# Two transformer blocks on one core: held weight chunks, a later norm product, and later down groups

## The chip, the core and the metric

The kernel runs on one core of a Trainium2 chip. The core has five engines that work side by side, each through its own list of instructions in order: PE (TensorE, the matrix products), DVE (VectorE), ACT (ScalarE), POOL (GpSimd) and SP (SyncE, which here issues the weight transfers). They wait for one another through semaphores. Matrix products are written to PSUM, eight banks of 512 fp32 columns; everything else lies in SBUF. The metric is the device time of one execution in microseconds (us).

## The reference, cut to what matters

Input: x of 256 tokens by 1024 features, fp32. Two different blocks follow each other, each two layers deep:

```
first block, per layer:
  x = x + concat(diff_attention, moba_attention)(rms_norm(x) @ w_in) @ w_out
  x = x + (silu(g) * up) @ w_down,   g, up = split(causal_conv3(rms_norm(x) @ w_up))
second block, per layer:
  x = x + 0.5 * (silu(h @ w_gate) * (h @ w_up)) @ w_down,   h = rms_norm(x)
  x = x + merged @ w_out     # forgetting attention and a gated linear recurrence, both
                             # from rms_norm(x) @ w_in, each gated by a sigmoid
  x = x + 0.5 * (the same feed-forward with other weights)
rms_norm(x) = x * rsqrt(mean(x^2) + 1e-6) * g
```

The feed-forward is 2816 wide in both blocks (22 pieces of 128). There are ten norms and six feed-forwards in all.

## The kernel before, in words

**Layout and products.** Activations are kept feature-major: X is four tiles that hold eight pieces of 128 features by 256 tokens. Each fp32 operand is split in two halves, high (rounded to the fast fp32 format) and low (the rest), and a product is two or three matmuls: high by high, high by low, low by high. The weight's high half (wh) is made by ScalarE, the low half (wl) by VectorE as raw minus wh. Names of tiles, as the profile shows them: raw, wh, wl for weights; xs for a norm's split input; as for a feed-forward's split activation; x for X; sq for the norm's squares and their running sum; st for the product that sums over features; rstd for the norm's factor; mm, mv and acc for PSUM banks of a projection, of a q/k/v projection with tokens as rows, and of a down contraction.

**The weight stream.** All weights are one list of chunks in the order of use (`phase_chunks`, line 176 on). A chunk is 128 by 1024 (one kind is slightly wider). `issue_dma` brings it into one of 7 raw buffers, `piece_h` and `piece_l` convert it in two halves of 512 columns into one of 5 buffers each for wh and wl (`RING = 5`). `next_chunk` takes the next one for use: it sets `st["done"]` to that chunk, and `h_open` lets a conversion be put in only for chunks below

```python
return c < st["dma"] and c < st["done"] + RING
```

so a chunk five further on, which goes into the same buffer, is opened only when the current one has moved on. What is put into an engine's list before the buffer is free waits there for the last matmul that reads it.

**The order of work.** It is written out when the kernel is built. A class `Estimate` keeps for each engine a planned time `T[engine]` and for each tile the time `R[tile]` at which it is planned ready. The main line issues PE's products; after each pair of matmuls `substep` runs `urgent` (weights that are nearly due), `tick` (units of background work: each is a generator that yields the engine and the tiles it waits for, and goes on once they are planned ready) and `fill` (conversions ahead). So a planned ready time decides where in PE's list a unit's matmuls stand. The real engines then run the lists in order.

**Norms.** `boundary` (line 720 on) is called as each piece of a residual sum is complete: it adds the piece to X, makes the split input of the next norm (`norm_tile`: high half on ScalarE, low half on VectorE), squares it on ScalarE and adds the square to the running sum on POOL (for the first norm on VectorE). After the eighth piece `norm_tail` (line 485 on) puts the two st matmuls into PE's list, once the sum is planned ready, and then the factor rstd = rsqrt (ScalarE and VectorE) and, where tokens must be scaled, two transposes (rt). The projections do not wait for rstd, since it is applied when a bank is emptied.

**Feed-forward.** `ffn` walks the order that `ffn_order(lag)` gives. "up" is a projection by two chunks, whose result is emptied, gated and split into an as tile. "dn" is one group of the down contraction: two as tiles by one chunk, into four of the eight output pieces (the first half). The groups of the first half come between the ups, each `lag` ups behind; the second half's groups come after all ups, and its last two groups are taken together. `lag` is 4 in the first block and 2 in the second.

**The last contraction.** In `down` and `down2` the last step takes its two chunks at once, as a list, and goes over the output pieces in the outer loop, so that pieces become complete one after the other:

```python
w = list(k_chunks(n, len(groups)))
for m in range(4):
    for i, h, l_ in w:
        one(i, m, h, l_)
```

By then `next_chunk` has been called twice, so `st["done"]` is the second chunk, while the first is read up to the last piece.

Of the kernel before, what the change touches and what calls it, by code (L numbers as in the profile page):

```python
# [144 lines left out]
def kernel(ctx: ExitStack, tc: tile.TileContext, t: dict):  # L145
    nc = tc.nc
    ctx.enter_context(tc.manual_schedule())
    est = Estimate()
# [31 lines left out]
    def phase_chunks():  # L180
        for l in range(L):
            wo = t["w_out"]
            at = {"dq0": 0, "dq1": 1, "mq0": 2, "mq1": 3, "dv0": 4, "mv0": 5}
            for step in MIX1.split():
                if step[1] == "o":
                    halves(wo[l, 2 * (step[0] == "m") + int(step[2])])
                else:
                    for i in range(2):
                        halves(t["w_p1"][l, at[step], i])
            ffn_chunks(t["w_up"], t["w_down"], l, 4)  # L190
        for l in range(L):
            ffn_chunks(t["w_gu1"], t["w_d1"], l, 2)
            wi = t["w_in2"]
            base = {"q": 0, "k": 4, "v": 8, "x": 12, "r": 16, "a": 20, "n": 24}
            for step in MIX2.split():
                if step == "q0":
                    halves(t["w_qf"][l])
                elif step == "G":
                    halves(t["w_g"][l])
                elif step in PAIRS:  # L200
                    for i in range(2):
                        halves(t["w_p2"][l, PAIRS.index(step), i])
                elif step[0] == "O":
                    half, g = divmod(int(step[1]), 2)
                    stream.extend(half_rows(t["w_out2"][l], half, 2 * g + i) for i in range(2))
                elif step[0] in "AR":
                    halves(t[{"A": "w_oa", "R": "w_or"}[step[0]]][l, int(step[1])])
                else:
                    halves(wi[l, base[step[0]] + int(step[1])])
            ffn_chunks(t["w_gu2"], t["w_d2"], l, 2)  # L210

    def halves(a):
        w = a.shape[-1] // 2
        stream.extend(a[:, i * w:(i + 1) * w] for i in range(2))
# [19 lines left out]
    def ffn_chunks(u, d, l, lag):  # L234
        for what, j in ffn_order(lag):
            if what == "up":
                halves(u[l, j])
            else:
                stream.extend(half_rows(d[l], j[0], g) for g in j[1])
# [14 lines left out]
    st = {"dma": 0, "h": 0, "l": 0, "use": 0, "done": 0}  # L254
# [90 lines left out]
    def W(eng, *aps):  # L345
        return (eng, aps)
# [138 lines left out]
    def norm_tail(N):  # L485
        while N.ss is None or N.ss[1] < KT:
            yield POLL
        ssum = N.ss[0]
        yield W("pe", ssum)
        while not bank_ok():  # L490
            yield POLL
        b = bank("st")
        pe.matmul(b[:, :S], ones_d, ssum, start=True, stop=True)
        yield W("act", b)
        r = blk("rstd")[:, :S]
        yield from rsqrt(r, b[:, :S], S)
        N.rstd = r
        if N.tok:

            yield W("pe", r)  # L500
            while not bank_ok():
                yield POLL
            b = bank("rt")
            for tt in range(2):
                pe.transpose(b[:, tt * P:(tt + 1) * P], r[:, tt * P:(tt + 1) * P], ident)
            yield W("dve", b)
            rt = small(4, "rt")
            dve.tensor_copy(rt[:, 0:2], b[:, 0:S:P])
            unbank()
            N.rt = rt  # L510

            yield W("dve", rt)
            dve.tensor_mul(rt[:, 2:4], rt[:, 0:2], rt[:, 0:2])
            yield W("dve", rt)
            dve.reciprocal(rt[:, 2:4], rt[:, 2:4])
            yield W("dve", rt)
            dve.tensor_scalar_mul(rt[:, 2:4], rt[:, 2:4], EPS)
            N.e2 = rt[:, 2:4]
# [55 lines left out]
    def k_chunks(n=KT, c=2):  # L574

        per = n // c
        for i in range(c):
            h, l_ = next_chunk(None)
            h3 = h.rearrange("p (k c) -> p k c", k=per)
            l3 = l_.rearrange("p (k c) -> p k c", k=per)  # L580
            for j in range(per):
                yield i * per + j, h3[:, j], l3[:, j]

    def proj(R):

# [82 lines left out]
    def down(acc, R, first, last, after=None):  # L668

        def one(k, m, h, l_):  # L670
            ms = slice(m * P, (m + 1) * P)
            mm3(as2(acc[m // 2])[:, m % 2], h[:, ms], l_[:, ms], R.high(k), R.low(k),
                first and k == 0 and m % 2 == 0, last and k == 1 and m % 2 == 1)

        if not last:
            for k, h, l_ in k_chunks(2):
                for m in range(KT):
                    one(k, m, h, l_)
                    substep()
        else:  # L680
            w = list(k_chunks(2))
            for p in range(4):
                for k, h, l_ in w:
                    for m in (2 * p, 2 * p + 1):
                        one(k, m, h, l_)
                        if k == 0:
                            substep()
                after(2 * p, [as2(acc[p])[:, 0]], False)
                after(2 * p + 1, [as2(acc[p])[:, 1]])
                substep()  # L690

    def down2(acc, R, groups, half_, first, last, after):

        n = 2 * len(groups)

        def one(i, m, h, l_):
            ms = slice(m * P, (m + 1) * P)
            mm2(acc[m], h[:, ms], l_[:, ms], R.both(2 * groups[i // 2] + i % 2), first and i == 0, last and i == n - 1)

        if not last:  # L700
            for i, h, l_ in k_chunks(n, len(groups)):
                for m in range(4):
                    one(i, m, h, l_)
                    substep()
        else:
            w = list(k_chunks(n, len(groups)))
            for m in range(4):
                for i, h, l_ in w:
                    one(i, m, h, l_)
                    if i < n - 1:  # L710
                        substep()
                after(4 * half_ + m, [hi(acc[m]), lo(acc[m])])
                substep()
# [24 lines left out]
    def ffn(N, evac, scale, N2, lag, mul):  # L738
        R = Ops(N.X)
        A = Ops([None] * NF)  # L740
        acc = [[], []]
        for what, j in ffn_order(lag):
            if what == "up":
                b = mul(R)
                spawn(evac(N, b if mul is proj else summed("u", b), j, A.tiles))
                substep()
            else:
                half_, groups = j
                wait_for(lambda: all(A.tiles[2 * g + i] is not None for g in groups for i in range(2)))
                first = not acc[half_]  # L750
                if first:
                    wait_for(lambda: bank_any(4))
                    acc[half_] = [bank("acc") for _ in range(4)]
                down2(acc[half_], A, groups, half_, first, NG - 1 in groups, boundary(scale, N2))
# [776 lines left out]
    norms = []  # L1531
# [7 lines left out]
    with tc.tile_pool(name="b1pool", bufs=1) as bp:  # L1539
        N0 = norms[0]  # L1540
        C = block1_consts(bp, N0)
        T.update(pe=T0 - 300.0, act=T0 - 700.0, dve=T0 - 200.0, pool=5000.0)
        for k in range(KT):
            a = blk("xs", F32R)
            act.activation(hi(a), xt(k), AF.Identity, scale=v1(N0.g, k))
            dve.scalar_tensor_tensor(lo(a), xt(k), v1(N0.g, k), hi(a).bitcast(F32), op0=ALU.mult, op1=ALU.subtract)
            piece_h()
            piece_l()
            N0.X[k] = a
        T["pe"] = T0 + 2000.0  # L1550
        for k in range(KT):
            add_squares(N0, squares(k))
        spawn(norm_tail(N0), front=True)
        for l in range(L):
            if l == 1:
                spawn(consts2())
            mix1(l, norms[2 * l], C, norms[2 * l + 1])
            ffn(norms[2 * l + 1], make_evac_conv(l), 1.0, norms[2 * l + 2], 4, proj)
    with tc.tile_pool(name="b2pool", bufs=1) as bp:
        C = block2_consts(bp)  # L1560
        for l in range(L):
            o = 4 + 3 * l
            ffn(norms[o], evac_swiglu, 0.5, norms[o + 1], 2, proj2)
            mix2(l, norms[o + 1], C, bp, norms[o + 2])
            ffn(norms[o + 2], evac_swiglu, 0.5, norms[o + 3], 2, proj2)
    wait_for(lambda: not active)


# [121 lines left out]
```

## Time and profile before

| what | value |
|---|---|
| time, median of three runs | 1904.14 us (1903.15 to 1908.57) |
| the profiled execution's own time | 1904.0 us |
| its span, first to last instruction | 1902.2 us |
| PE busy | 1865.8 us |
| DVE busy | 1534.8 us |
| ACT busy | 1271.2 us |
| POOL busy | 63.5 us |
| mean granted TensorE clock | 0.995 |

Busy time is the union of an engine's instructions; waiting is not in it. Nearly every instruction shows line 112, that of the helper which records it, so the tiles' names tell the work apart. "Idle before" in a row is the time the engine stood still just before the instruction, with the engine, line and tile that ended the wait.

### The profile page before, as it was taken

The numbers are of one execution on the slowest core, as the hardware profiler recorded it, in microseconds if no ns is written. First come the engines' busy times: TensorE is split into PE (matmuls) and PEld (weight loads), VectorE is DVE, ScalarE is ACT, GpSimd is POOL, SyncE is SP. The second block draws the span as 40 slices with busy tenths as digits, with TensorE's granted clock in tenths as the row PEclk, the third lists the DMA queues.
The fourth block names the chain that finished last, engine by engine and source line by source line (L and its number), as shares of the span: only waits on it lengthen the run. The fifth ranks groups of instructions, "written<-read, shape, count | busy, mean of one in ns | idle before, by whom it ended". The sixth has DMA issues, their size and how long they took to land.

```text
span 1902.2 us, 32094 instructions
## 1 busy us (share of the span) xinstructions
PE 1865.8 (98%) x11446; PEld 1657.9 (87%) x11446; DVE 1534.8 (81%) x3284; ACT 1271.2 (67%) x3099; POOL 63.5 (3%) x91
## 2 busy tenths in 40 slices
PE   9999999999999999999999999999999999999998
PEld 7899997889999888888888888888888888888887
DVE  7879886888988777779969877767776898898775
ACT  7866665876666666567788666556655778866653
POOL 2010001001000000000000100010001000000000
PEclk9999999999999999999999999999999999999999
DMA  9446655444655566655556566656666455565662
GB/s 288 150 144 194 188 182 160 138 153 135 210 186 175 182 188 188 189 193 162 157 177 192 187 191 187 186 169 190 187 185 210 157 161 172 189 197 188 189 188 82
DMA packets 113153, 339.76 MB, mean 179 GB/s; under 512 B 10796, under 2 KB 11860, under 8 KB 112480
## 3 DMA queue, kind: packets, MB, share of 16 engines
q1 hardware_dynamic: 111392, 330.21, 55.4%
q0 software_dynamic: 1456, 7.47, 1.4%
q8 instruction: 90, 1.47, 0.3%
q14 instruction: 71, 0.58, 0.1%
q10 hardware_dynamic: 144, 0.02, 0.0%
HBM read 336.30 MB, written 1.36 MB: 178 GB/s over the span
## 4 chain that ended last, share of the span: by engine, by line
PE 89%; DVE 7%; ACT 2%; DMA 1%; issue 1%; POOL 0%; POOLq 0%; SPq 0%; ACTq 0%
PE mm L112 49%; PE acc L112 22%; PE mv L112 12%; DVE wl L112 2%; PE av L112 2%; PE s L112 1%; DMA raw<-in_w_p 1%; ACT wh L112 1%; DVE x L112 1%; PE qt L112 1%; PE pt L112 1%; PE g L112 1%; DVE xs L112 1%; DVE z L112 0%; PE st L112 0%
## 5 line engine op out<-in xcount | busy, mean ns | idle before, releaser
L112 DVE TENSOR_TENSOR wl<-raw,wh 128x512 fp32r<-128x512 f32 x1248 | 819.1, 688 | 216.6 <-ACT wh L112 192.4
L112 ACT ACTIVATE wh<-raw 128x512 fp32r<-128x512 f32 x1248 | 718.3, 628 | 317.0 <-PE mm L112 101.7
L112 PE MATMUL mm<-xs,wh 128*128 128x256 f32 (+1 forms) x2816 | 753.4, 340 | 6.8 <-DVE xs L112 4.8
L112 PE MATMUL mm<-xs,wl 128*128 128x256 f32 x2112 | 596.7, 283 | 0.0
L112 PEld LDWEIGHTS mm<-xs,wh 128*128 128x128 f32 x2816 | 485.5, 190 | 70.0 <-DVE xs L112 6.5
L112 PEld LDWEIGHTS mm<-xs,wl 128*128 128x128 f32 x2112 | 401.2, 190 | 0.2
L112 PE MATMUL acc<-as,wh 128*128 128x512 f32 x1056 | 372.4, 394 | 5.4 <-DVE as L112 5.4
L112 PE MATMUL acc<-as,wl 128*128 128x256 f32 x1056 | 297.1, 281 | 0.0
L112 PE MATMUL mv<-wh,xs 128*128 128x512 f32 (+2 forms) x832 | 255.8, 388 | 0.4 <-DVE xs L112 0.4
L112 PEld LDWEIGHTS acc<-as,wh 128*128 128x128 f32 x1056 | 198.2, 188 | 51.5 <-DVE as L112 7.3
L112 PEld LDWEIGHTS acc<-as,wl 128*128 128x128 f32 x1056 | 198.7, 188 | 0.0
L112 PE MATMUL mm<-hS,wh 128*128 128x512 f32 x512 | 180.9, 395 | 0.0
L112 PEld LDWEIGHTS mv<-wh,xs 128*128 128x128 f32 x832 | 149.9, 191 | 28.2 <-DVE xs L112 0.8
L112 PE MATMUL mv<-wl,xs 128*128 128x512 f32 (+2 forms) x416 | 157.8, 379 | 0.0
L112 PE MATMUL mm<-hS,wl 128*128 128x256 f32 x512 | 143.9, 281 | 0.0
L112 ACT ACTIVATE u<-mm 128x256 f32<-128x256 f32 x176 | 63.9, 383 | 92.1 <-PE mm L112 92.0
L112 DVE TENSOR_TENSOR u<-mm,u 128x256 f32<-128x256 f32 x176 | 67.8, 423 | 61.5 <-ACT u L112 61.3
L112 PEld LDWEIGHTS mm<-hS,wh 128*128 128x128 f32 x512 | 96.1, 188 | 21.1
L112 POOL TENSOR_TENSOR sq<-sq,sq 128x256 f32<-128x256 f32 x63 | 50.2, 797 | 1578.4 <-ACT sq L112 1577.1
L112 PEld LDWEIGHTS mm<-hS,wl 128*128 128x128 f32 x512 | 96.4, 188 | 0.1
L112 PEld LDWEIGHTS mv<-wl,xs 128*128 128x128 f32 x416 | 79.4, 191 | 14.8
L112 DVE SCALAR_TENSOR_TENSOR y<-u,vec,y 128x255 f32<-128x255 f32 (+1 forms) x176 | 80.8, 481 | 3.1
(210 smaller groups left out, 2225.6 us busy)
## 6 DMA issues: line engine op xcount, KB each, us to landing
raw<-in_w_gu SPq DMA_DIRECT2D x176, 512.0 KB, 4.3
raw<-in_w_up SPq DMA_DIRECT2D x88, 512.0 KB, 4.1
raw<-in_w_d SPq DMA_DIRECT2D x88, 512.0 KB, 4.4
raw<-in_w_p SPq DMA_DIRECT2D x84, 512.0 KB, 4.6
raw<-in_w_in SPq DMA_DIRECT2D x68, 512.0 KB, 3.7
raw<-in_w_down SPq DMA_DIRECT2D x44, 512.0 KB, 4.1
raw<-in_w_out SPq DMA_DIRECT2D x32, 512.0 KB, 4.2
raw<-in_w_oa SPq DMA_DIRECT2D x16, 512.0 KB, 4.0
```

The costliest lines, as they stand in the source:

```text
L112: f(*a, **k)
```

## The change

It has three parts. The order `ffn_order` is asked for with a lag of 6 instead of 4 in the first block and of 4 instead of 2 in the second, in the list of chunks and in the walk alike. In `norm_tail` the running sum's planned ready time is raised by 1500 ns before the unit waits for it, so that the st matmuls stand later in PE's list. And the two places that take their chunks as a list do so by a new function, which sets `st["done"]` back to the first of them until the next chunk is called for.

```diff
-            ffn_chunks(t["w_up"], t["w_down"], l, 4)
+            ffn_chunks(t["w_up"], t["w_down"], l, 6)
...
-            ffn_chunks(t["w_gu1"], t["w_d1"], l, 2)
+            ffn_chunks(t["w_gu1"], t["w_d1"], l, 4)
...
-            ffn_chunks(t["w_gu2"], t["w_d2"], l, 2)
+            ffn_chunks(t["w_gu2"], t["w_d2"], l, 4)
...
         ssum = N.ss[0]
+        est.R[ssum.name] += 1500.0
         yield W("pe", ssum)
...
+    def held_chunks(n, c):
+
+        first = st["use"]
+        w = list(k_chunks(n, c))
+        st["done"] = first
+        return w
...
-            w = list(k_chunks(2))
+            w = held_chunks(2, 2)
...
-            w = list(k_chunks(n, len(groups)))
+            w = held_chunks(n, len(groups))
...
-            ffn(norms[2 * l + 1], make_evac_conv(l), 1.0, norms[2 * l + 2], 4, proj)
+            ffn(norms[2 * l + 1], make_evac_conv(l), 1.0, norms[2 * l + 2], 6, proj)
...
-            ffn(norms[o], evac_swiglu, 0.5, norms[o + 1], 2, proj2)
+            ffn(norms[o], evac_swiglu, 0.5, norms[o + 1], 4, proj2)
...
-            ffn(norms[o + 2], evac_swiglu, 0.5, norms[o + 3], 2, proj2)
+            ffn(norms[o + 2], evac_swiglu, 0.5, norms[o + 3], 4, proj2)
```

## Rows read from the trace of the kernel before

**Rows 1.** The page's first two parts: busy time, and tenths in 40 slices.
```profile
PE 1865.8 (98%) x11446; PEld 1657.9 (87%) x11446; DVE 1534.8 (81%) x3284; ACT 1271.2 (67%) x3099; POOL 63.5 (3%) x91
...
PEclk9999999999999999999999999999999999999999
```

**Rows 2.** Waits of PE: engine, tile, waited for: us in total, times, longest us.
```profile
PE st L112 <- POOL sq L112: 12.8, 7, 2.4
PE acc L112 <- DVE as L112: 5.4, 6, 1.1
PE mm L112 <- DVE xs L112: 4.8, 6, 1.2
PE mm L112 <- DVE sp L112: 2.6, 2, 1.3
PE mm L112 <- ACT xs L112: 2.0, 2, 1.0
...
PE qt L112 <- DVE qn L112: 2.0, 2, 1.7
PE mv L112 <- DVE xs L112: 0.4, 2, 0.2
PE rt L112 <- DVE rstd L112: 0.3, 1, 0.3
```

**Rows 3.** Timeline of PE, 634 to 641: start us, duration us, instruction [idle before].
```profile
634.04 0.39 PE L112 MATMUL mm<-xs,wh 128*128 128x512 f32 x1
...
637.04 0.28 PE L112 MATMUL mm<-xs,wl 128*128 128x256 f32 x1
637.16 0.40 PE L112 MATMUL mm<-xs,wh 128*128 128x512 f32 x1
...
638.97 0.28 PE L112 MATMUL mm<-xs,wl 128*128 128x256 f32 x1
640.87 0.70 PE L112 MATMUL st<-sq,cst 128*128 128x256 f32 x2 [1.62 <-POOL sq L112]
```

**Rows 4.** Windows: stretch, length, busy by engine, PEclk, DMA share, GB/s.
```profile
130.80:134.10 3.30, 3.30 (x16) 3.30 (x17) 3.30 (x8) 2.27 (x7) 2.40 (x4) 0.50 0.00 0
...
1274.20:1277.50 3.30, 3.30 (x13) 2.82 (x12) 2.22 (x5) 3.27 (x7) 0.00 (x0) 0.50 0.57 168
```

**Rows 5.** Timeline of ACT over the same boundary.
```profile
633.42 1.15 ACT L112 ACTIVATE wh<-raw 128x512 fp32r<-128x512 f32 x2 [3.74 <-PE acc L112]
...
639.06 0.51 ACT L112 ACTIVATE xs<-x,vec 128x256 fp32r<-128x256 f32 x1 [0.37 <-DVE x L112]
```

**Rows 6.** Timeline of DVE over the same boundary.
```profile
638.15 0.88 DVE L112 TENSOR_TENSOR x<-acc,x 128x256 f32<-128x256 f32 x2
```

**Rows 7.** Groups of instructions: count | busy us, mean ns | idle before, releasers.
```profile
L112 DVE TENSOR_TENSOR wl<-raw,wh 128x512 fp32r<-128x512 f32 x1248 | 819.1, 688 | 216.6 <-ACT wh L112 192.4 <-PE acc L112 14.0 <-PE qt L112 0.6
L112 ACT ACTIVATE wh<-raw 128x512 fp32r<-128x512 f32 x1248 | 718.3, 628 | 317.0 <-PE mm L112 101.7 <-issue 93.7 <-PE acc L112 85.5
...
L112 ACT ACTIVATE sq<-x 128x256 f32<-128x256 f32 x80 | 31.5, 402 | 0.0
```

**Rows 8.** Timeline of DVE, 1268 to 1273; POOL added from 1267.90 to 1268.64.
```profile
1267.96 0.96 DVE L112 SCALAR_TENSOR_TENSOR xs<-x,vec,xs 128x256 fp32r<-128x256 f32 x1
...
1270.24 0.48 DVE L112 SCALAR_TENSOR_TENSOR xs<-x,vec,xs 128x256 fp32r<-128x256 f32 x1
```

**Rows 9.** Instructions on tile sq, POOL: duration ns min/median/max, first and last start.
```profile
L112 POOL TENSOR_TENSOR sq<-sq,sq x63: 722/742/1082, 129.4 to 1715.3; 128x256 f32<-128x256 f32 x63
```

**Rows 10.** The chain that ended last, in time: start us, us, what (first down group, two ups).
```profile
659.70 2.81 PE acc L112 x16
662.51 11.14 PE mm L112 x64
```

**Rows 11.** Timeline of PE, at the last group of a first half.
```profile
789.45 0.50 PE L112 MATMUL acc<-as,wh 128*128 128x512 f32 x1 [1.01 <-DVE as L112]
```

**Rows 12.** Windows, columns as in rows 4: block 1, ups alone before the first down.
```profile
139.60:166.90 27.30, 27.30 (x231) 27.27 (x230) 25.70 (x54) 20.38 (x41) 0.00 (x0) 1.00 0.55 178
```

## The prediction

> **What bounds the kernel now.** I read the page first: its busy row has PE (TensorE) at 98% of the span with VectorE at 81% and ScalarE at 67%, and the granted clock's row stands at nine tenths or more in every slice [rows 1]. So the time is PE's own work plus the little in which PE stands still or runs slowly, and a change that leaves PE's instructions as they are can only win or lose there. Next the waits of PE, the one view that names the standing still [rows 2]: 12.8 us in seven waits of the norm's sum product (st) for POOL, 5.4 us in six of a down contraction (acc) for VectorE's low half of an activation (as), 4.8 us in six and 2.0 us in two of an up projection (mm) for the split input (xs), 0.4 us in two of a q/k/v projection (mv) for it. That is 25.4 us in 23 waits. The rows for sp, qn and rt (4.9 us) I count as staying.
>
> Idle understates what a wait costs, because the matmul before it is still draining when the wait begins. Between starts a low product is followed by the next high one after 0.12 us (637.04 to 637.16); across a wait it was 1.90 us (638.97 to 640.87), so 1.78 us were lost where 1.62 us of idle were counted [rows 3]: 0.16 us more per wait, an estimate that I apply to all 23 (3.7 us).
>
> Last the stretches by granted clock: six times, each behind a group of these waits, PE ran a stretch of 3.3 us at 0.50 of the clock, which is 1.2 GHz; the first and the last are shown [rows 4]. Work at half the rate there costs 1.65 us each, 9.9 us in all.
>
> **Where the waits come from.** At the end of a contraction ScalarE stood 3.74 us before a weight piece (wh) at 633.42, waiting for PE's acc [rows 5]. The piece belongs to the chunk five after the first of the two that the last contraction holds; it goes into that first chunk's buffer, and PE reads it until the end. The input splits (xs) of the residual tiles stand behind it in ScalarE's order: the last began at 639.06 [rows 5]. On VectorE the piece's low half (wl) stood likewise ahead of the residual sums (x), the last of which began at 638.15 [rows 6], although the next projection's first matmul had started at 634.04 [rows 3]. POOL's additions for the norm follow those, and st follows POOL. One pattern, at all nine ends of a contraction that feed a norm.
>
> **held_chunks.** It adds and removes no instruction. It keeps the piece for that buffer from being put into ScalarE's order until the next chunk is called for, which is after the contraction's last matmul in program order. So ScalarE's 3.74 us wait goes at nine places, and with it xs and x come when their acc is ready. From the end of the contraction the last tile then needs four steps: x (0.88 us, [rows 6]), xs high (0.51 us, [rows 5]), the square (0.40 us, [rows 7]) and the last addition (0.72 to 1.08 us, [rows 9]) in sequence, with 0.5 us for hand-overs as an estimate, are 3.0 to 3.4 us; the low half of xs (0.48 to 0.96 us, [rows 8]) is ready no later. PE gets to the xs tile that it needs last only at seven eighths of the first projection: a stretch of two ups is 11.14 us [rows 10], so one is 5.57 us and seven eighths are 4.9 us. All waits for xs (7.2 us in ten) go, and most of the st ones would go by this alone, since st stood 4.25 us of PE's work behind the end (634.04 to 639.09, the low product's 0.12 us included [rows 3], less 0.8 us for the one wait for xs between, the mean in [rows 2]).
>
> What is late next: the conversion of the postponed chunk, two wh of 0.628 us and two wl of 0.688 us [rows 7], 2.6 us of work on two engines. Its cover is the three chunks converted ahead: a chunk is 2.81 us of PE's time [rows 10], so it is due 8.4 us after the end. Cost taken 0; without that cover 2.6 us at nine places, 24 us. A gain below nothing I exclude, since its work stays.
>
> **The norm's sum product 1500 ns later.** One line in norm_tail moves the two st matmuls of ten norms back in PE's order by 1.5 us of planned work; what hangs on them (logarithm, exponential, square, three VectorE operations, and where tokens are scaled two transposes) moves with them. The wait before st at 640.87 was 1.62 us [rows 3] and the longest 2.4 us [rows 2]; with the earlier xs and 1.5 us of projection put before st, none of the seven stays. Who now waits for the norm's factor: the evacuations of block 1's ups and of q, k and v, which hold PSUM banks. Eight banks stand against one bank per 5.6 us, so 1.5 us take none more. The cost lies between 0 and 1.5 us in ten norms (15 us); I take 1 us for handed-on waits in the middle of the program, near the lower end, because the factor's time on the clock stays (st ran 1.78 us late before). At the start there is no st wait to win, and PE did wait 2.0 us in two for qn [rows 2], a tile that by the code needs that st's factor: between 0 and 1.5 us, and I take 1.
>
> *A rule that speaks against it.* The xs low half took 0.96 us where a POOL addition ran beside it and 0.48 us where none did [rows 8]; POOL's own additions run from 722 to 1082 ns [rows 9]. The Trainium skill (Trainium Architecture — The Big Picture, What this means for kernel authors) says that VectorE and GpSimd contend for one shared port pair by an exclusive lock and not by a split of bandwidth. The trace agrees in sign. If the denser boundary slowed each of seven additions from the median of 742 ns to the longest, 0.34 us each, the sum would by that rule be ready up to 2.4 us later, at about 5.8 us; st then stands 4.25 + 1.5 = 5.75 us behind the end, so by rule and by row alike next to nothing is lost.
>
> **More ups before the first down (4 to 6, and 2 to 4).** Same chunks, same matmuls; the first half's down groups come two ups later, and one more group (16 matmuls, 2.81 us [rows 10]) stands between the last up and the group that needs its activation. The wait there is 1.01 us at 789.45 [rows 11], one of six. 2.81 us is over twice the longest of the six (1.1 us [rows 2]), so all six go: 5.4 + 6 x 0.16 = 6.4 us. Against it: a longer stretch of ups alone, where VectorE is fullest. In block 1's opening ups it was busy 25.70 of 27.30 us with PE busy throughout [rows 12], so two more ups keep a margin of 6%. Cost 0; if VectorE were instead over PE by the same 6%, 0.7 us for 11.4 us of ups, in two layers 1.4 us. DMA transfers are reordered alike and are as many, on the same queue.
>
> **Sum.** 6.4 us (down) + 17 other waits at 20.0 + 17 x 0.16 = 22.7 us + clock 9.9 us = 39.0 us of gain, less 2 us of cost: 37 us off the profiled execution's 1904.0 us (span 1902.2 us and 1.8 us around it; the median of the runs shown, 1904.14 us, is the same). That gives 1867 us. If a wait in ten survives, 1870; without the 2 us, 1865. Its own range is 1860 to 1874.
>
> **Rivals.**
> The clock stays as it is. The waits go, but some smaller ones stay, and they bring six half-rate stretches as before: 1867 + 9.9 = 1877 us. For it: PE still waits for sp and qn [rows 2]. Against: those were not among the six places. Chance 0.17, up to 1885 with some st waits left.
>
> The wait is handed on. st is no longer waited for, but the users of the norm's factor are, by as much: seven waits of 13.9 us and the clock's 9.9 come back, 1867 + 13.9 + 9.9 = 1891 us. For it: ten norms move with all their chain. Against: the only such wait now is 0.3 us, of rt for rstd [rows 2]. Or held_chunks merely lets the next piece block ScalarE in the same place; then the lag's 6.4 us alone are won, 1898 us. Together 0.06, about half of it too near 1904 to be told apart.
>
> The weights come late, the slower side. The postponed chunk stands behind xs, squares and the table work on ScalarE, and the next chunk behind it: PE would wait for wl in the second up after each of nine ends. With the clock's stretches kept, the time is 1877 + 9 w for a wait of w: slower than before from w = 3.0 us, and 1924 us at two chunks' conversion (5.2 us). For it: VectorE is at 94% there [rows 12]. Against: PE waits nowhere for wh or wl now [rows 2], and the cover is 8.4 us. Chance 0.04.
>
> **How the numbers follow.** The forecast has 0.73. The range 1860 to 1885 takes in the first rival and leaves out the other two and the tails of the first cases. A difference of 0.3% (5.7 us) is about what a measurement of this kernel can tell: faster 0.73 + 0.17 + 0.03 = 0.93, the same 0.03, slower 0.04.
>
> **What would show it.** In the profile after: no wait of wh for acc near 3.7 us at a contraction's end that feeds a norm; last xs within about 3 us of the end; no rows st <- POOL sq, acc <- DVE as and mm <- DVE xs among PE's waits, or under 1 us each; granted clock 1.00 behind the boundaries; PE's busy work unchanged in count. Wrong it would be if PE waits for wl or for rstd, if as waits remain, or if new stretches at 0.50 appear in the middle of a feed-forward.

## The result, and the profile after

The changed kernel took 1863.16 us (median of four runs, 1862.71 to 1865.8) against 1905.27 us for the kernel before beside it (1903.15 to 1908.57). The ratio is 0.978 with a 95% interval of 0.9763 to 0.9798: a gain of 42 us, where 37 were forecast. The profiled span fell from 1902.2 to 1861.4 us, 40.8 us.

First the busy row and the granted clock's row of the page of the changed kernel, to be held against [rows 1].

```profile
PE 1850.7 (99%) x11446; PEld 1649.2 (89%) x11446; DVE 1530.4 (82%) x3284; ACT 1272.2 (68%) x3099; POOL 63.1 (3%) x91
...
PEclk9999999999999999999999999999999999999999
```

PE executes as many instructions as before, but in 15.1 us less, and the other 25.7 us of the 40.8 are time in which PE stood still. The view by core (span, mean granted clock) gives the clock, 0.995 before:

```profile
core 0: 1861.4 us, clock 1.000
```

So the 15.1 us of busy time are, by the prediction's figures, mostly the half-rate stretches (9.9 us) and the drain that idle does not count (3.7 us); 1.5 us I do not assign. The waits of PE in the changed kernel (tile, waited for: us in total, times, longest), all of them, against [rows 2]:

```profile
PE mm L112 <- DVE sp L112: 2.6, 2, 1.3
PE warm L1004 <- DVE vp L112: 2.0, 1, 2.0
PE qt L112 <- DVE qn L112: 1.4, 2, 1.2
PE mv L112 <- DVE wl L112: 0.2, 1, 0.2
PE mm L112 <- DVE xs L112: 0.2, 1, 0.2
```

The st and as rows are gone, and of the xs rows one of 0.2 us is left. What stays is what stayed in the forecast: sp, and at the start qn (an attention's normed queries and keys) and vp (zeros that PE's first products read; it stood at 2.0 us before as well). New is 0.2 us for wl, at 20.51, at the start too.

The same boundary as in [rows 3, 5, 6], now near 620 us. Timelines of PE, ACT, DVE and POOL of the changed kernel (start us, duration us, instruction [idle before <- releaser]):

```profile
620.12 0.39 PE L112 MATMUL mm<-xs,wh 128*128 128x512 f32 x1
...
624.88 0.28 PE L112 MATMUL mm<-xs,wl 128*128 128x256 f32 x1
625.00 0.60 PE L112 MATMUL st<-sq,cst 128*128 128x256 f32 x2
```
```profile
619.84 0.51 ACT L112 ACTIVATE xs<-x,vec 128x256 fp32r<-128x256 f32 x1 [0.58 <-DVE x L112]
...
621.33 0.51 ACT L112 ACTIVATE xs<-x,vec 128x256 fp32r<-128x256 f32 x1 [0.68 <-DVE x L112]
...
622.06 3.23 ACT L112 ACTIVATE wh<-raw 128x512 fp32r<-128x512 f32 x6
```
```profile
620.43 0.87 DVE L112 TENSOR_TENSOR x<-acc,x 128x256 f32<-128x256 f32 x2
...
622.71 3.89 DVE L112 TENSOR_TENSOR wl<-raw,wh 128x512 fp32r<-128x512 f32 x6 [0.34 <-ACT wh L112]
```
```profile
622.29 0.74 POOL L112 TENSOR_TENSOR sq<-sq,sq 128x256 f32<-128x256 f32 x1 [0.75 <-ACT sq L112]
```

ACT's first conversion (wh) now stands behind the last xs and its square, and waits for nothing. The last xs starts 1.21 us behind the next projection's first matmul, against 5.02 us before. The contraction's last product started 0.11 us ahead of that matmul, and the squares' sum is ready at 623.03 (622.29 + 0.74), 3.0 us after that last product; st stands 4.88 us behind the first mm, without a wait and with 1.97 us to spare.

At the as waits the chain of waits answers to [rows 10, 11]. Columns: start, length, work. Up and down groups follow unbroken, and the second half's groups run in one piece:

```profile
754.70 11.18 PE mm L112 x64
765.88 39.04 PE acc L112 x224
804.92 4.74 PE mv L112 x39
```

Last two windows (stretch, length, busy by engine, PEclk, DMA share, GB/s): the boundary near 130 us, where [rows 4] had 0.50, and all of block 1's ups after it up to the first down group, which answer to [rows 12].

```profile
124.00:143.00 19.00, 18.76 (x154) 18.30 (x153) 17.42 (x33) 13.74 (x32) 5.96 (x7) 1.00 0.48 152
137.50:174.60 37.10, 37.10 (x314) 37.10 (x313) 34.28 (x70) 27.88 (x57) 0.00 (x0) 1.00 0.56 182
```

The clock is 1.00 behind the boundary, and over the longer stretch of ups VectorE is busy 34.28 of 37.10 us with PE busy throughout.

### The profile page after: what moved, and what is told of

Its sections match the earlier page's. It is cut to its first block, busy times and chain, and to the rows that moved or that the text cites. A ratio compares the mean times of both kernels' runs of the same rounds, so it can differ in the third digit from the quotient of the medians.

```text
span 1861.4 us, 32089 instructions
## 1 busy us (share of the span) xinstructions
PE 1850.7 (99%) x11446; PEld 1649.2 (89%) x11446; DVE 1530.4 (82%) x3284; ACT 1272.2 (68%) x3099; POOL 63.1 (3%) x91
## 4 chain that ended last, share of the span: by engine, by line
PE 93%; DVE 4%; DMA 1%; ACT 1%; issue 0%; SPq 0%; ACTq 0%
PE mm L112 51%; PE acc L112 24%; PE mv L112 13%; PE av L112 2%; PE s L112 1%; DMA raw<-in_w_p 1%; DVE wl L112 1%; PE qt L112 1%; PE pt L112 1%; PE g L112 1%; DVE xs L112 1%; DVE z L112 0%; DVE sg L112 0%; DVE ya L112 0%; DVE yc L112 0%
## 5 line engine op out<-in xcount | busy, mean ns | idle before, releaser
L112 PEld LDWEIGHTS acc<-as,wh 128*128 128x128 f32 x1056 | 198.2, 188 | 44.4
```

Source lines behind the costliest of these rows:

```text
L112: f(*a, **k)
```

## The experiments

Theory A is the prediction's: ScalarE's wait for the held buffer is the one cause of the st and xs waits, the lag is the cause of the as waits, and the half-rate stretches follow these waits. The rivals are named in the texts put on record. Each ratio is against the kernel before on the same chip.

**One part alone.** e1 is the kernel before with `held_chunks` and its two uses, e2 with the lags, e3 with the planned 1500 ns.

```diff
 e1:
-            w = list(k_chunks(n, len(groups)))
+            w = held_chunks(n, len(groups))      # and the same for down
 e2:
-   ..., 4, proj)   ..., 2, proj2)
+   ..., 6, proj)   ..., 4, proj2)               # and the same in the list of chunks
 e3:
         ssum = N.ss[0]
+        est.R[ssum.name] += 1500.0
```

> The kernel before with held_chunks alone. Theory A (the blocked conversion on ScalarE is the cause, the 1500 ns a reserve): PE's ten waits for xs (7.2 us of idle) go, the seven st waits fall from 12.8 us to 3 us at most, the half-rate stretches go; the six waits for as (5.4 us) stay. Time 1905 less 32 to 36, about 1869 to 1874 us. Theory B (the 1500 ns is what frees st): st waits stay at 6 us or more and some half-rate stretches with them; 1880 to 1888 us.

e1 took 1876.27 us, ratio 0.9832 (0.9819 to 0.9846): 32 us less than the kernel before on this chip (1908.33). The time is 2 us above the range expected, which was reckoned from 1905. Its waits of PE, all but vp's:

```profile
PE acc L112 <- DVE as L112: 5.4, 6, 1.1
PE qt L112 <- DVE qn L112: 5.1, 1, 5.1
PE mm L112 <- DVE sp L112: 2.6, 2, 1.3
...
PE st L112 <- DVE sq L112: 1.1, 1, 1.1
PE mm L112 <- DVE xs L112: 0.2, 1, 0.2
```

All seven st waits for POOL are gone with this part alone, and of the ten xs waits one of 0.2 us is left; no half-rate stretch is left in the middle, although the six as waits of up to 1.1 us are all there. The one st wait, for VectorE's sum, is the first norm's, at the start, where a wait of 5.1 us for qn and a half-rate stretch stand too. How near a wait of st was in the middle, POOL and PE of e1 at the same boundary show:

```profile
630.66 0.83 POOL L112 TENSOR_TENSOR sq<-sq,sq 128x256 f32<-128x256 f32 x1 [0.44 <-ACT sq L112]
```
```profile
631.91 0.59 PE L112 MATMUL st<-sq,cst 128*128 128x256 f32 x2
```

The sum is there 0.42 us ahead of st, against 1.97 us in the changed kernel. A sum that was 1.6 us late is thus 0.4 us early without the 1500 ns.

> The kernel before with the longer lags alone. Both theories: the six as waits go, 5.4 us of idle and 6.4 us of time, 1899 us; waits for st and xs and the half-rate stretches stay. If the clock's stretches hung on the as waits too, some of the six would go and the time would be 1892 to 1896 us.

e2 took 1897.46 us, ratio 0.9941 (0.9928 to 0.9955). The as row is gone and every boundary wait is as before. The gain of 10.9 us is more than the 6.4 expected. The half-rate stretches of the middle were four instead of six, which is 3.3 us by the prediction's 1.65 us each; why two fewer came, the runs do not show. At its start e2's profile has a stretch of 6.8 us at half the rate (44.1 to 50.9) that the profile of the kernel before does not have.

> The kernel before with the 1500 ns alone. Theory A: ScalarE still stands 3.7 us at nine ends, so the xs waits stay or grow (7 us or more), and the st waits shrink from 12.8 us to 2 us or less since st stands 1.5 us later; the sum of both stays above 8 us, and half-rate stretches stay in part: 1886 to 1896 us. Theory B: the st waits were what cost, so most of the 42 us comes: 1870 to 1878 us.

e3 took 1893.37 us, ratio 0.9922 (0.9908 to 0.9935). Its waits of PE, those that concern the change:

```profile
PE mm L112 <- DVE xs L112: 7.4, 10, 1.2
PE acc L112 <- DVE as L112: 5.4, 6, 1.1
...
PE mm L112 <- ACT xs L112: 2.0, 2, 1.0
...
PE rt L112 <- DVE rstd L112: 1.7, 2, 0.9
...
PE mv L112 <- DVE xs L112: 1.6, 4, 0.6
PE rt L112 <- DVE spe L112: 1.1, 1, 1.1
PE st L112 <- POOL sq L112: 1.0, 1, 1.0
```

And ACT at the boundary, where the cause stands as before ([rows 5] at 633.42):

```profile
633.23 1.15 ACT L112 ACTIVATE wh<-raw 128x512 fp32r<-128x512 f32 x2 [3.74 <-PE acc L112]
```

Of 12.8 us of st waits 1.0 are left, but the xs waits grew from 7.2 us in ten (4.8, 2.0 and 0.4) to 11.0 in 16, and rt waits came. This is the handed-on wait of the prediction's second rival, in a kernel where the late sum itself is not mended: st is late because xs is late, and moving st puts the xs wait in its place. Only about half of it was handed on (of the 11.8 us that st lost, 3.8 came back at xs and 2.5 at rt), and the half-rate stretches of the middle were two instead of six, so e3 still won 15.0 us. The three parts' gains alone (32.1, 10.9 and 15.0 us) do not add up to the 42, since the hold and the 1500 ns win the same waits.

**Leaving one part out.** e4 is the changed kernel without the 1500 ns; e5 is the changed kernel without the hold.

```diff
 e4:
-        est.R[ssum.name] += 1500.0
 e5, in held_chunks:
-        st["done"] = first
```

> The changed kernel without the 1500 ns. Theory A: st waits of 3 us at most in all, 1863 to 1867 us, not to be told from the changed kernel by more than 0.2%. Theory B: st waits of 6 us or more and half-rate stretches: 1873 to 1882 us.

e4 took 1868.11 us, ratio 0.9788 (0.9773 to 0.9802), 1 us above the range expected. No st wait of a boundary, no as wait, no half-rate stretch in the middle. Against e1, on the same chip, the lags are worth 8.2 us (1876.27 less 1868.11).

> The changed kernel without held_chunks. Theory A: ScalarE stands 3.7 us at nine ends again; waits for xs of 10 to 12 us and for rt of 1.7 us and some half-rate stretches, no as waits; 1908 less 15 for the 1500 ns less 6 to 11 for the lags, 1882 to 1888 us, some 20 us slower than the changed kernel. Theory B (the 1500 ns and the lags do it): under 1872 us.

e5 took 1886.26 us, ratio 0.9891 (0.9874 to 0.9907), as Theory A had it: the xs waits of e3 are there (8.1 us in twelve for mm), the as waits are not, and a stretch at half the rate is again behind the boundary, 133.9 to 137.3. Without the hold 22.1 us of the gain are missing (1886.26 against e7's 1864.15, same chip).

**The start.** e7 is the changed kernel again, as the measure for e5, e6 and e8. e8 leaves the 1500 ns out at the first norm alone.

```diff
 e8:
-        est.R[ssum.name] += 1500.0
+        if N is not norms[0]:
+            est.R[ssum.name] += 1500.0
```

> The changed kernel once more, beside the three that follow and the kernel before on the same chip. Ratio to the kernel before 0.978 to 0.981 as the first time; PE's waits between the start and the end only those for sp (2.6 us); the start's waits (for qn, st or wl) anywhere from 1.4 to 6 us, since the weight transfers there landed up to 4 us apart from run to run.

> The changed kernel with the 1500 ns left out for the first norm alone. Theory A1 (the 1500 ns acts at the start and nowhere else, by taking st out of the way of the projections there): 2 to 4 us slower than the changed kernel on the same chip, with st waiting 1 to 1.7 us for DVE near 19 us. Theory A2 (the 1500 ns does nothing, and what differs at the start is the transfers): within 1.5 us of it.

e7 took 1864.15 us, ratio 0.9775 (0.9761 to 0.979); e8 1867.57 us, 0.9793 (0.9779 to 0.9808). The ratios' intervals overlap, but each of e8's four runs (1865.88 to 1868.67) is above each of e7's (1862.25 to 1865.33).

Where the two differ, the first product of the first contraction shows: it parts the start from all that follows. Its row (count: duration ns min/median/max, first to last start us; shape) in the kernel before, e1, e4 and the changed kernel:

```profile
L112 PE MATMUL acc<-oS,wh x256: 274/282/386, 99.9 to 440.9; 128*128 128x256 f32 x128
L112 PE MATMUL acc<-oS,wh x256: 274/282/387, 105.4 to 438.8; 128*128 128x256 f32 x128
L112 PE MATMUL acc<-oS,wh x256: 274/282/390, 103.6 to 435.7; 128*128 128x256 f32 x128
L112 PE MATMUL acc<-oS,wh x256: 274/282/386, 99.5 to 431.6; 128*128 128x256 f32 x128
```

From that first start to the end of the span (1902.2, 1875.1, 1865.4 and 1861.4) the four profiles take 1802.3, 1769.7, 1761.8 and 1761.9 us. So in the middle the hold is worth 32.6 us, the lags beside it 7.9 us, and the 1500 ns beside both nothing (0.1 us). e7, e11 and e8 take 1762.0, 1761.9 and 1761.9 us there as well: e8 and e7 differ at the start alone, 105.0 against 101.5. PE in e8 at the start:

```profile
19.36 0.70 PE L112 MATMUL st<-sq,cst 128*128 128x256 f32 x2 [0.97 <-DVE sq L112]
...
45.97 3.21 PE L112 MATMUL qt<-cst,qn 128*128 128x128 f32 x12 [3.70 <-DVE qn L112]
```

In the changed kernel st stands at 20.85 without a wait, and qn was waited for by 1.16 us:

```profile
43.20 0.33 PE L112 MATMUL qt<-cst,qn 128*128 128x128 f32 x1 [1.16 <-DVE qn L112]
```

So on this chip the version with the 1500 ns at the start was faster, by 3.4 us by these medians (4.0 us by e4 against e7 across two chips), and this is all that the line is worth beside the other two parts. The sum of the first norm is VectorE's, not POOL's, and was 1.0 to 1.7 us late for st in e1, e4 and e8. How st's wait would lengthen the later wait for qn is not shown. The chain of waits leads from qn to a weight transfer (start, us), in e7 and then in e8:

```profile
27.66 12.84 DMA raw<-in_w_p
29.25 13.86 DMA raw<-in_w_p
```

It landed at 40.5 and 43.1 us; by the same rows at 40.1 in the changed kernel, 42.5 in e4 and 44.4 in e1, and qn's wait grows with it (1.16 us, 1.97 in e7, then 3.27 in e4, 3.70 in e8, 5.12 in e1). But it landed at 40.1 in the kernel before too, without the 1500 ns and without a wait of st. So the rival that the landing differs by itself is not excluded as a part of the 3.4 us; against it stand the four runs each.

**The cover of the weights.** e6 holds one chunk more, so that two chunks instead of three are converted ahead.

```diff
 e6, in held_chunks:
-        st["done"] = first
+        st["done"] = first - 1
```

> The changed kernel with st[done] set one chunk further back in held_chunks, so that one chunk fewer is converted ahead at nine ends (about 5.6 us of PE's work as cover in place of 8.4 us). If the cover is ample, as forecast: no PE wait for wl or wh, time within 2 us of the changed kernel. If the cover was nearly used up (the slower rival's place): waits for wl of 1 us or more at several ends, 1870 us or more.

e6 took 1873.00 us, ratio 0.9824 (0.981 to 0.9839), 8.9 us over e7. It was not the weights: PE waits for wl once, 1.4 us at the start, and nowhere at a boundary. So the time came out as expected of late weights, and the cause did not. The loss stands in a row mm <- DVE xs of 6.7 us in six. DVE, then PE, of e6:

```profile
134.28 0.98 DVE L112 TENSOR_TENSOR wl<-raw,wh 128x512 fp32r<-128x512 f32 x1 [1.39 <-ACT wh L112]
135.18 0.74 DVE L112 TENSOR_TENSOR x<-acc,x 128x256 f32<-128x256 f32 x2
```
```profile
136.77 0.39 PE L112 MATMUL mm<-xs,wh 128*128 128x256 f32 x1 [1.69 <-DVE xs L112]
```

A chunk that is nearly due by the plan is put in at once, here in the middle of the boundary. VectorE stands 1.39 us before its low half, with the residual sum x behind it, and PE waits for xs. The kind of loss is that of the kernel before, an instruction that waits in an in-order list with the boundary's work behind it, though it waits for another engine and not for a buffer. So the cover carries the change in this form: with a chunk less of it the conversion comes back into the boundary. That the conversion is put in as urgent I read from the code and its place in the rows; no run isolates it.

**Beyond the change.** e11 is the changed kernel beside e9 and e10. e9 plans the landing of chunks 14 to 17 later, as the trace has it, and puts none of them in as urgent before that; e10 adds an edit for the sp waits, which holds VectorE's products of the attention's gate until the recurrence's four outputs, which the sp projection reads, have been put into its list; e12 is the changed kernel with that edit alone.

```diff
 e9:
-        est.R[r.name] = T["dma"] + 2200.0
+        est.R[r.name] = T["dma"] + 2200.0 + {14: 7000.0, 15: 9500.0, 16: 11000.0, 17: 11000.0}.get(c, 0.0)
...
-                if not h_open():
+                c = st["h"] // NP
+                if not h_open() or (13 < c < 18 and est.R[raws[c].name] > max(T["act"], T["pe"])):
                     return
 e10 (with e9's) and e12 (alone):
+    def ya_unit(x, sg, M, j, R):
+        while not (x.ready and sg.ready and R.no == 4):
...
+            spawn(ya_unit(summed("ya", b), ga[j], M, j, R))
```

> The changed kernel with the planned landing of weight chunks 14 to 17 put 7 to 11 us later, and no urgent conversion of them before it. If the wait for qn at the start comes from VectorE standing before such a chunk's low half (wl, 3.1 us in the changed kernel) with the norm factor's small steps behind it, qn is ready before the chunk lands: no wait for qn, no half-rate stretch there, 1 to 5 us less than the changed kernel. If the transfers themselves set the start, the wait only changes its name (mv for wl) and the time is the same within 1 us.

> The one before, with the products of ya by its gate held back until the last of the recurrence's split tiles (sp) is in the order. If sp is late because two such products (0.6 us each) stand between it and its input on VectorE, the two waits for sp shrink from 2.6 us to under 0.5 us in all: 2 to 3 us less. If the chain through the scan is late by itself, they stay.

> The changed kernel, as the measure for the two that follow on the same chip: waits for sp (2.6 us) and at the start for qn (1.4 to 2.2 us), 1862 to 1866 us.

e11 took 1865.88 us, ratio 0.9778 (0.9765 to 0.9791); e9 1871.68 us, 0.9812 (0.9798 to 0.9825); e10 1870.48 us, 0.9803 (0.9789 to 0.9816). e9 failed, 5.8 us over e11: the wait for qn went, and others came. Two of the waits of PE in e9, then DVE at the start, then PE at the end of the first attention (jk is a scratch tile of its last head), and two windows:

```profile
PE qt L112 <- DVE jk L112: 2.3, 1, 2.3
PE s L112 <- DVE sm L112: 2.0, 2, 1.9
```
```profile
49.33 0.29 DVE L112 CUSTOM_DVE_ANT_0 p<-s,biasT 128x128 f32<-128x128 f32 x1 [3.51 <-DMA biasT<-ext]
```
```profile
131.77 0.73 PE L112 MATMUL qt<-cst,jk 128*128 128x128 f32 x2 [2.29 <-DVE jk L112]
```
```profile
50.60:60.60 10.00, 10.00 (x38) 7.64 (x39) 7.32 (x37) 9.86 (x62) 0.00 (x0) 0.50 0.49 184
129.00:135.80 6.80, 4.51 (x22) 4.25 (x22) 3.41 (x9) 3.08 (x11) 0.00 (x0) 0.50 0.01 2
```

At the start VectorE stood 3.51 us before a bias transfer, and a longer stretch than in e7 ran at half the rate, 1.2 GHz: one wait less there showed the next. The wait for jk is not at the start; it came at 131.77, with a second stretch at half the rate around it. Why the edit brought it the runs do not show. e10 keeps these losses, though its sp row is gone.

> The changed kernel with the held-back gate products alone, the start as in the changed kernel. No waits for sp, as in the run before (2.6 us of idle, 2.9 us of time with the drain): ratio to the kernel before 0.976 to 0.977, where the changed kernel had 0.9775 to 0.978; that difference is near what five rounds can tell. If the gate products only move the wait to yr or to the last down contraction, the ratio stays at 0.978.

e12 took 1862.48 us, ratio 0.976 (0.9747 to 0.9774), and its waits of PE have no sp row. It is the best version measured, but its interval overlaps those of the changed kernel (0.9775 and 0.9778 on other chips), so a gain over it is not shown by the times. Its profile is 2.4 us shorter from the first contraction on (1759.5 against 1761.9 us), where the sp row stood for 2.6 us.

## Why the prediction was right

**What bounds the kernel** held: PE's instructions stayed as they were, and the gain lay in its standing still (25.7 us of span) and its slow stretches.

**held_chunks** held. The 3.74 us that ScalarE stood, which the prediction put at all nine ends, were 3.7 to 3.9 us at seven of them; at the other two (behind the second block's attentions) the piece stood 2.0 and 2.1 us. After, no wait of wh for acc as long as 2 us is left, xs and x came when acc was ready, and the sum was ready 3.0 us behind the contraction's last product (3.0 to 3.4 forecast). "Most of the st ones would go by this alone" was all of them (e1): the 32.6 us that the sum gives the waits at the boundaries and the clock (22.7 and 9.9) are what the hold alone won in the middle. Of the 4.25 us by which st was to stand behind the end, 3.48 were left in e1 (631.91, with the next projection's first matmul at 628.43); that its planned place moved with the conversions is likely, but not shown. The margin was 0.42 us. The cost of 0 for the postponed conversion held, and e6 shows that the cover is needed, though what fails without it is the order in the boundary and not the weight's arrival; the prediction's third rival had the wrong mechanism and only the right place.

**The 1500 ns** had its two costs mis-sized. The 1 us for handed-on waits in the middle was nothing: no row of rt for rstd is left after, and e4 without the line takes as long there as the changed kernel. The 1 us at the start did not come either: the profiles before and after reach the first contraction at 99.9 and 99.5 us, and e8 loses 3.4 us to e7 without the line, so on that chip the cost had the wrong sign. I saw no st wait at the start in the kernel before and took a later st to be a loss. In the middle the line is reserve: with the hold, st is not late without it (e1, e4), and that this part would be needed for the st waits the runs do not bear out.

**The lag** had its six waits right and its price too low: 6.4 us forecast, 8.2 us by the medians of e4 against e1 and 7.9 us in the middle of their profiles. Idle plus 0.16 us per wait leaves out 1.5 us over the six; I have not shown where these lie. VectorE's margin in the longer stretch of ups held (34.28 of 37.10 us).

**The clock** held: no stretch at half the rate is left in the middle of the changed kernel, though sp waits of 1.3 us stay, so the first rival falls. e1 and e4 have none there either, while e2, e3 and e5, which keep waits at the boundaries, have four, two and one. In the middle of these runs the stretches came only at boundaries with waits, never behind the single as waits of up to 1.1 us. But not each such boundary brought one: in the kernel before PE waited 0.62 and 1.62 us at 1080.53 and 1083.12, with a stretch behind, and 0.61 and 1.62 us at 638.29 and 640.87 with none. What decides between them the runs do not show, so the count of six was read off the trace and not derived.

**The rule that speaks against it**: the clash of VectorE with POOL stayed as it was (the longest xs low half is 1.06 us, its median 0.49; POOL's additions average 791 ns, 797 before), and made no sum late.

The two kernels are 42.1 us apart by the medians, 5.1 more than forecast. In the middle of the profiles they are 40.4 us apart where the sum had 39.0 before its costs: 1.4 us more, the lag's 1.5 less 0.1. The two costs of 1 us that did not come are 2 us more. The 1.7 us that are left lie between the medians and these two profiles; they are less than the width of the interval (0.35% of 1905 is 6.7 us), and I do not assign them.

## What to carry to other kernels

When an engine at 98% waits for a chain of small steps, follow the chain back to the first instruction that waits for a buffer: in an in-order list one early conversion, put in 3.7 us before its buffer was free, held up everything behind it, and moving only that was worth 32 of 42 us. Moving the last link instead (e3) handed about half of the wait on to its neighbours and won 15 us. Bound a "later" edit by its slack at every place where it acts, the start too: the same 1500 ns was idle reserve at nine norms and, by e7 and e8, gain at the tenth. And part a trace where the noise ends: here all that follows the first contraction's first product agrees to 0.1 us between three profiles of one kernel, while the start differs by 4 us.

## What the runs showed of the hardware

The start of one and the same kernel is not one trajectory: the first wait for qn was 1.16 us, 1.97 us and none in three profiles of the changed kernel, and a half-rate stretch there came in one of them (e7, 44.9 to 48.3) and not in the others. The first contraction began at 99.5, 101.5 and 97.6 us, and what follows took 1761.9, 1762.0 and 1761.9 us. In e1 a stretch of the start was at 0.50 that takes in the end of the wait of 5.1 us for qn (until 47.25); the same stretch of the changed kernel, shown first, had 1.00:

```profile
44.60:51.20 6.60, 6.60 (x46) 5.09 (x46) 5.47 (x15) 6.46 (x38) 0.00 (x0) 1.00 1.02 353
44.60:51.20 6.60, 3.83 (x16) 3.36 (x17) 6.07 (x12) 4.23 (x7) 0.00 (x0) 0.50 1.02 347
```

A few us between two versions at the start can therefore be told only by several runs, as e7 and e8.
